# A hybrid decoder trunk: the cast of each weight block prepared ahead waits for the mark that releases the next load

## The chip, the cores and the metric

The kernel runs on one core of a Trainium2 chip. The metric is the time of one execution on the device in microseconds (us), as the median of several runs. Engines are called by the profile's names: PE (matrix engine), PEld (its weight loads), DVE (vector), ACT (scalar), POOL (GpSimd) and SP (here only a queue of DMAs). Each engine takes its own queue in order.

## The reference

The program computes two layers on x of 1024 tokens by 1024 features, all in float32:

```
for i in range(2):
    mix = hgrn2_mixer(x, ...) if i == 0 else conformer_conv_mixer(x, ...)
    x = layer_norm(ALPHA * x + mix, ln_mix_g[i], ln_mix_b[i])
    ff = jnp.square(jax.nn.relu(x @ ffn_w1[i])) @ ffn_w2[i]
    x = layer_norm(ALPHA * x + ff, ln_ffn_g[i], ln_ffn_b[i])
```

The first mixer is a gated linear recurrence with four projections and an output projection. The second has a pointwise projection to 2048 features, a sigmoid gate, a causal depthwise convolution of 31 taps, a layer norm, a silu and a second pointwise projection. Each MLP goes from 1024 to 4096 features and back. What must be seen here is that the order of the work is: mixer A, first MLP (up, down), mixer B (pointwise, convolution, pointwise), second MLP.

## The kernel before, in words

**Products.** Every float32 operand of a large product is split into a high half (a cast to the narrower type fp32r, on ACT) and a low half (the operand less its high half, a subtraction on DVE). PE then makes three products: high by high, high by low, low by high. A slot of 8 KB in each partition holds both halves, `slot[:, 0]` high and `slot[:, 1]` low.

**The first MLP.** Its two matrices are multiplied by a seven-product scheme for 2x2 blocks of blocks; the forms (sums of blocks) are taken in the order `ORDER = (1, 2, 6, 5, 7, 3, 4)`. In the up part (class `Up`, PE's `ps<-x1f,fw`) there are 8 columns c of 7 forms, each of 24 matmuls of 128x512. A product's result leaves PSUM by a copy `c` on ACT (L1266) or by an addition on DVE. In the down part (`down_all`, PE's `ps<-dw,dh`) the outer loop goes over the forms, the inner one over 8 blocks c, again 24 matmuls each, six for each of four row groups `gi`. Behind the last block of a form the four sums are accumulated into `y` (`into`), in two tiles of four token rows. The last form, 4, does its first two blocks alone and the other six together by `gi`; in it rows of `y` are normalised (`to_conv`), transposed on PE (`turn`: four transposes into a PSUM bank, then a cast on ACT and a subtraction on DVE into `xa`) and become the input of the pointwise product that follows.

**Weights prepared ahead.** During the first MLP the kernel also splits 38 blocks of weights of later stages, 512 KB each, and stores both halves to HBM (`ready`), so that they can be loaded as they are. The function `spare` (L1434 to L1452) does one step of it. It is called at the end of a form's split (`Slots.count`, L95 to L99), in the up part for 3 forms of 8 and in the down part for 6 of 8. There is one slot `spare` and one load buffer `next`, claimed behind the first column of the up part. A step has these parts:

- the mark: a DVE copy (L1440) of one element of the low half just made into `now`, a small tile of the tag `ss`, of which there are four buffers in turn;
- if a block has been loaded: its cast on ACT (L1443), its subtraction on DVE, and the two stores by SP (L1447);
- if blocks are left: a POOL copy of the mark into the first column of `next` (L1450), and SP's load into `next` (L1451), which is thereby held until the mark is made and the previous block is out of `next`.

So the mark paces the loads. The memory of `spare` and `next` is given to other tiles when the down part ends.

**Other users of the queues.** POOL also issues the DMAs that add up blocks of weights in `sum_w` (L421, L423) during the up part; each such issue waits for the DMA before it. SP's queue carries the loads of `dr` (raw weights of the down part), of `dh` (its already split activations, then split again from `hf`), and the stores of `ready`.

**What sets the order.** All instructions are recorded and then ordered for each engine by a scheduler that estimates when each could run. An instruction added at one place can therefore shift the order of others on every engine.

Of the kernel before, what the change touches and what calls it, by code (L numbers as in the profile page):

```python
# [268 lines left out]
def body(ctx, tc, d, out):  # L269
    nc = tc.nc  # L270
# [1163 lines left out]
    def spare(after):  # L1434

        if not hold:
            return
        slot, raw = hold
        now = stat.tile([P, 2, 4], F32, tag="ss", name="ss")[:, 0, :1]
        nc.vector.tensor_copy(out=now, in_=after)  # L1440
        if staged:
            key = staged.pop()
            nc.scalar.copy(out=slot[:, 0].bitcast(F32R), in_=raw)  # L1443
            vector.tensor_tensor(out=slot[:, 1].bitcast(F32R), in0=raw, in1=slot[:, 0], op=ALU.subtract)
            ready[key] = tuple(dram.tile([P, 1024], F32, name=f"ready{len(ready)}_{i}") for i in range(2))
            for i in range(2):
                nc.sync.dma_start(out=ready[key][i], in_=slot[:, i])  # L1447
        if ahead:
            name, at = ahead.pop(0)
            nc.gpsimd.tensor_copy(out=raw[:, :1], in_=now)  # L1450
            nc.sync.dma_start(out=raw, in_=d[name][at])  # L1451
            staged.append((name, at))  # L1452

    fw = Forms(nc, vector, slots((144, 152, 48, 112, 120), "fw"), raws(run(192, 4, 4)), raws(run(160, 2, 4), "sum"), spare, 3, range(44))
    fw.todo = [[(blocks("w1q", 0, c), 2 if c < 2 else 0)] for c in range(NFC)]
    up = Up()
# [24 lines left out]

    y = [view(32 + 16 * h, (NTB, D), F32, "y") for h in range(2)]
    fw = Slots(nc, vector, slots([112, 120, 144, 152, 128, 136, 168], "dw"), raws([192, 196, 200, 204, 160, 164], "dr"), spare, 6, range(10, 50))
    fh = Slots(nc, vector, slots([0, 8, 16, 24, 96, 104, 176], "dh"))
    g, b = gain(184, "ln_ffn", 0)
# [472 lines left out]
```

## Time and profile before

| | before |
|---|---|
| median of 3 runs | 2057.86 us (2054.11 to 2058.38) |
| the profiled execution | 2059.69 us |
| its span in the profile | 2057.9 us |
| granted clock of PE, mean | 0.998 |
| first MLP, up part | about 513 to 828 us of the span |
| first MLP, down part | 827.88 to 1136.09 us |
| first pointwise product of mixer B | from 1136.09 us |

A row of a timeline gives the start, the length, the engine, the line, the operation, output and inputs, shape and count of a group of like instructions; in brackets stands how long the engine had been idle before it and what ended that, in us. L204 is a helper through which most instructions go, so those groups are told apart by the names of their tiles. In a window's row each engine's busy time has its number of instructions behind it. A group of waits gives, after the two sides of the wait, the sum of the idle time in us, how often, and the longest.

### The profile page before, as it was taken

To read this page: it belongs to the slowest core of one execution; us is meant where nothing else is said; L and a number is where in the kernel's file an instruction comes from. 1 tells how busy PE (TensorE), PEld (TensorE's weight loads), DVE (VectorE), ACT (ScalarE), POOL (GpSimd) and SP (SyncE) were. 2 spreads that over 40 slices of the span, in tenths; PEclk is the share of its full clock that TensorE was granted. 3 is DMA by queue.
4 is the path that set the end of the run, shared out by engine and by line. 5 is a ranking of instruction groups with operands and counts; after the bars stand their busy time and mean duration, and the time that the engine had idled before them with its cause. 6 is when DMAs were issued, how large, how long until landed. Compare 5 with 4: busy or idle time off the path is not lost. (4 is left out here: it accounts for less than half of the span.)

```text
span 2057.9 us, 29631 instructions
## 1 busy us (share of the span) xinstructions
PE 2026.5 (98%) x11144; PEld 1670.6 (81%) x11144; DVE 1487.4 (72%) x1978; ACT 1092.0 (53%) x1725; POOL 392.1 (19%) x393
## 2 busy tenths in 40 slices
PE   8999999999999999999999999999999999999998
PEld 7888887788787888888888888888888887888886
DVE  8698887877966665666567898889589666754456
ACT  5456565631654555444443776488625555443343
POOL 0112222111100000000001699079110000100002
PEclk9999999999999999999999999999999999999999
DMA  4788989842689786999998854587759778995542
GB/s 187 221 200 228 261 240 252 268 187 82 180 295 307 243 286 224 372 338 325 338 336 301 308 185 184 194 330 272 255 215 343 241 231 297 392 294 197 194 154 102
DMA packets 183944, 517.55 MB, mean 251 GB/s; under 512 B 17912, under 2 KB 49784, under 8 KB 182776
## 3 DMA queue, kind: packets, MB, share of 16 engines
q1 hardware_dynamic: 168312, 456.93, 61.8%
q0 software_dynamic: 15488, 58.72, 12.3%
q8 instruction: 87, 1.43, 0.3%
q14 instruction: 57, 0.47, 0.1%
HBM read 380.85 MB, written 201.85 MB: 283 GB/s over the span
## 5 line engine op out<-in xcount | busy, mean ns | idle before, releaser
L204 PE MATMUL ps<-dw,dh 128*128 128x512 f32 x2688 | 611.1, 389 | 0.0
L204 PEld LDWEIGHTS ps<-dw,dh 128*128 128x128 f32 x2688 | 504.2, 188 | 104.6 <-DVE dh L204 0.2
L204 PE MATMUL ps<-x1f,fw 128*128 128x512 f32 x1344 | 309.7, 392 | 4.6 <-ACT c L1266 2.5
L204 PEld LDWEIGHTS ps<-x1f,fw 128*128 128x128 f32 x1344 | 252.5, 189 | 60.3 <-ACT c L1266 3.6
L204 PE MATMUL ps<-xf,fs 128*128 128x512 f32 x1008 | 250.0, 399 | 3.7 <-issue 2.0
L204 POOL TENSOR_TENSOR cb<-cb,prod 128x512 f32<-128x512 f32 x168 | 223.1, 1337 | 12.5 <-ACT prod L1589 2.0
L204 DVE TENSOR_TENSOR dh<-dh 128x1024 fp32r<-128x1024 f32 x112 | 136.5, 1222 | 116.1 <-ACT dh L72 112.7
L204 PEld LDWEIGHTS ps<-xf,fs 128*128 128x128 f32 x1008 | 185.1, 189 | 43.3 <-issue 2.2
L204 DVE SCALAR_TENSOR_TENSOR ps<-u,par,ps 128x512 f32<-128x512 f32 x296 | 206.1, 749 | 11.0 <-ACT ps L1601 9.5
L204 PE MATMUL ps<-xa,wa 128*128 128x512 f32 x864 | 203.0, 392 | 0.1
L72 ACT CAST dh<-dh 128x1024 fp32r<-128x1024 f32 x112 | 117.4, 1051 | 156.0 <-DMA dh<-hf 148.9
L204 PEld LDWEIGHTS ps<-xa,wa 128*128 128x128 f32 x864 | 160.3, 188 | 33.2 <-ACT ha L1331 0.3
L72 ACT CAST dw<-dr 128x1024 fp32r<-128x1024 f32 x112 | 117.3, 1052 | 131.0 <-PE ps L204 115.3
L204 DVE TENSOR_TENSOR dw<-dr,dw 128x1024 fp32r<-128x1024 f32 x112 | 136.3, 1222 | 69.5 <-ACT dw L72 68.4
L1589 ACT ACTIVATE prod<-u,par 128x512 f32<-128x512 f32 x168 | 119.8, 726 | 37.1 <-POOL cb L204 36.7
L518 POOL TENSOR_TENSOR mv<-mv,nhalf 128x1 f32<-128x1 f32 x32 | 42.2, 1321 | 404.8 <-DVE mv L204 394.5
L1450 POOL COPY next<-ss 128x1 f32<-128x1 f32 x38 | 18.9, 497 | 414.5 <-DVE spare L204 255.1
L204 PE MATMUL ps<-w,oT 128*128 128x512 f32 x384 | 89.9, 392 | 1.3 <-ACT oT L932 0.8
L204 PE MATMUL ps<-xb,wa 128*128 128x512 f32 x384 | 91.1, 393 | 0.0
L204 DVE TENSOR_TENSOR spare<-next,spare 128x1024 fp32r<-128x1024 f32 x38 | 46.5, 1224 | 60.4 <-ACT spare L1443 60.3
L204 PE MATMUL ps<-vw,xf 128*128 128x512 f32 x336 | 79.9, 400 | 5.9 <-ACT vw L435 5.3
L204 PEld LDWEIGHTS ps<-w,oT 128*128 128x128 f32 x384 | 71.4, 188 | 16.6 <-ACT oT L932 1.2
(249 smaller groups left out, 2955.9 us busy)
## 6 DMA issues: line engine op xcount, KB each, us to landing
wa<-ready SPq DMA_DIRECT2D x140, 512.0 KB, 4.6
dh<-hf SPq DMA_DIRECT2D x112, 512.0 KB, 5.0
sum_w<-in_w_dram POOLq DMA_DIRECT2D x40, 1024.0 KB, 10.6
ready<-spare SPq DMA_DIRECT2D x76, 512.0 KB, 5.3
raw<-in_w1q_dram SPq DMA_DIRECT2D x66, 512.0 KB, 4.4
dr<-sum_w SPq DMA_DIRECT2D x64, 512.0 KB, 5.7
hf<-ht SPq DMA_DIRECT2D x112, 256.0 KB, 5.1
dr<-in_w_dram SPq DMA_DIRECT2D x48, 512.0 KB, 4.6
```

The costliest lines, as they stand in the source:

```text
L72: self.nc.scalar.copy(out=slot[:, 0, c], in_=raw[:, c])
L204: return op(*args, **kw)
L518: nc.gpsimd.tensor_tensor(out=dst, in0=src, in1=nhalf[:, :n], op=ALU.pow)
L1450: nc.gpsimd.tensor_copy(out=raw[:, :1], in_=now)
L1589: nc.scalar.activation(tp, u[:, k : k + HT], AF.Copy, scale=tap(j, k))
```

## The change

One line is added in `spare`, as the first of the part that deals with a loaded block:

```
         if staged:
             key = staged.pop()
+            nc.gpsimd.tensor_copy(out=slot[:, 0, :1], in_=now)
             nc.scalar.copy(out=slot[:, 0].bitcast(F32R), in_=raw)
             vector.tensor_tensor(out=slot[:, 1].bitcast(F32R), in0=raw, in1=slot[:, 0], op=ALU.subtract)
```

POOL copies the mark into the first column of the slot's high half. The cast that follows overwrites that column, so it has to come after the copy, and the copy after the mark. It also has to come after the store of the block that was in the slot. Lines behind it are one higher in the changed kernel: the load's copy is L1451, the load L1452. There are 38 such copies more on POOL, one for each block.

On POOL, first MLP, up part, before (`sum_w` are the blocks added up by DMA, `next<-ss` the copy that lets a load go):

```order
L423 DMA sum_w_5415<-sum_w_5415 128x1024 x2
L1450 COPY next<-ss 128x1 x3
L421 DMA sum_w_5882<-in_w_dram 128x2x1024
L1450 COPY next<-ss 128x1
L423 DMA sum_w_5882<-sum_w_5882 128x1024 x2
```

On POOL at the same place, changed (`spare<-ss` is the copy that lets a cast go):

```order
L421 DMA sum_w_5885<-in_w_dram 128x2x1024
L1443 COPY spare<-ss 128x1
L1451 COPY next<-ss 128x1
L423 DMA sum_w_5885<-sum_w_5885 128x1024
L1443 COPY spare<-ss 128x1
L423 DMA sum_w_5885<-sum_w_5885 128x1024
L1451 COPY next<-ss 128x1
```

The copies for casts now stand between the issues of `sum_w` too.

On DVE, end of the first MLP's down part, before. The rows begin at the first accumulation into `y` behind form 3; `dw_7171` is the slot of the second block of form 4, `ss_8674` and `ss_8712` are marks, `mv`, `bs` the statistics of the normalisation:

```order
L204 TENSOR_TENSOR y_7168<-y_7168,ps_70 128x512 x2
L204 TENSOR_TENSOR spare_5428<-next_5429,spare_5428 128x1024
L204 BN_STATS bs_9006<-y_7168 128x6
L204 BN_STATS bs_9214<-y_7168 128x6
L204 TENSOR_SCALAR mv_8998<-mv_8998 128x1
L204 TENSOR_TENSOR y_7169<-y_7169,ps_70 128x512
L1440 COPY ss_8674<-dw_7171 128x1
L204 BN_AGGR mv_9009<-bs_9006 128x2
L204 TENSOR_TENSOR y_7169<-y_7169,ps_70 128x512
L204 TENSOR_TENSOR dh_7197<-dh_7197 128x1024
L1440 COPY ss_8712<-dw_7172 128x1
L204 TENSOR_TENSOR dw_7171<-dr_7184,dw_7171 128x1024
```

On DVE at the same place, changed. Here `dw_7193` and `dw_7183` are the slots of the first and second block of form 4; the first eleven rows from the first accumulation into `y`:

```order
L204 TENSOR_TENSOR y_7180<-y_7180,ps_70 128x512
L204 TENSOR_TENSOR dw_7193<-dr_7195,dw_7193 128x1024
L204 TENSOR_TENSOR y_7180<-y_7180,ps_70 128x512
L204 TENSOR_SCALAR mv_9036<-mv_9036 128x1
L204 BN_STATS bs_9044<-y_7180 128x6
L204 BN_STATS bs_9252<-y_7180 128x6
L204 TENSOR_TENSOR y_7181<-y_7181,ps_70 128x512
L204 BN_AGGR mv_9047<-bs_9044 128x2
L204 TENSOR_SCALAR mv_9036<-mv_9036 128x1
L204 SCALAR_TENSOR_TENSOR y_7180<-y_7180,mv_9036,ln_ffn_g_7213 128x1024
L204 TENSOR_TENSOR y_7181<-y_7181,ps_70 128x512
```

And the eleven behind them, to the subtraction that makes the low half of `dw_7183`:

```order
L204 TENSOR_SCALAR mv_9047<-mv_9047 128x1
L204 SCALAR_TENSOR_TENSOR y_7180<-y_7180,mv_9047,ln_ffn_g_7213 128x1024
L204 TENSOR_TENSOR spare_5428<-next_5429,spare_5428 128x1024
L204 TENSOR_TENSOR dh_7209<-dh_7209 128x1024
L204 SCALAR_TENSOR_TENSOR y_7180<-y_7180,mv_9036,ln_ffn_b_7215 128x1024
L204 SCALAR_TENSOR_TENSOR y_7180<-y_7180,mv_9047,ln_ffn_b_7215 128x1024
L204 TENSOR_TENSOR dh_7210<-dh_7210 128x1024
L1440 COPY ss_8711<-dw_7183 128x1
L204 TENSOR_TENSOR dh_7212<-dh_7212 128x1024
L204 TENSOR_TENSOR xa_7219<-ps_70,xa_7219 128x4x128
L204 TENSOR_TENSOR dw_7183<-dr_7196,dw_7183 128x1024
```

This subtraction was the 13th instruction from the first accumulation and is now the 22nd. Behind it come another subtraction for `xa`, one for `spare`, a third for `xa`, two marks, and then the subtraction for the next block, `dw_7184`.

On PE at this place, before (`dw_7181` and `dw_7171` are the first two blocks of form 4, the others the six that are taken together; `ident,y` are transposes):

```order
L204 MATMUL ps_70<-dw_7181,dh_7200 128x512 x24
L204 MATMUL ps_70<-dw_7171,dh_7192 128x512 x24
L204 MATMUL ps_70<-dw_7172,dh_7193 128x512 x9
L204 MATMUL ps_70<-dw_7174,dh_7194 128x512 x6
L204 MATMUL ps_70<-dw_7175,dh_7195 128x512
L204 MATMUL ps_70<-dw_7172,dh_7193 128x512 x5
L204 MATMUL ps_70<-dw_7174,dh_7194 128x512 x6
L204 MATMUL ps_70<-dw_7175,dh_7195 128x512
L204 MATMUL ps_70<-dw_7172,dh_7193 128x512 x2
L204 MATMUL ps_70<-ident_74,y_7168 128x128 x8
```

On PE at this place, changed (`dw_7191` is the last block of form 3):

```order
L204 MATMUL ps_70<-dw_7191,dh_7210 128x512 x24
L204 MATMUL ps_70<-dw_7193,dh_7212 128x512 x20
L204 MATMUL ps_70<-dw_7183,dh_7204 128x512 x4
L204 MATMUL ps_70<-ident_74,y_7180 128x128 x12
L204 MATMUL ps_70<-dw_7183,dh_7204 128x512 x19
L204 MATMUL ps_70<-ident_74,y_7180 128x128 x4
L204 MATMUL ps_70<-dw_7183,dh_7204 128x512
L204 MATMUL ps_70<-dw_7184,dh_7205 128x512 x8
L204 MATMUL ps_70<-dw_7186,dh_7206 128x512 x6
```

The first transposes of `y` moved from behind 30 matmuls of the third to fifth block into the second block. Over the whole down part PE's order was 1230 matmuls, 8 transposes, 31, 8, 57, 8, 24, 8 and 2 matmuls; it is now 1180, 12, 19, 4, 86, 8, 30, 8 and 29.

More of the change, by code (lines that the diff above doesn't have):

```diff
@@ L1442, in spare @@
             key = staged.pop()
+            nc.gpsimd.tensor_copy(out=slot[:, 0, :1], in_=now)
             nc.scalar.copy(out=slot[:, 0].bitcast(F32R), in_=raw)
```

## The prediction

> **What bounds the kernel now.** I read the page first. PE, the matrix engine, carries the time:
>
> ```profile
> span 2057.9 us, 29631 instructions
> PE 2026.5 (98%) x11144; PEld 1670.6 (81%) x11144; DVE 1487.4 (72%) x1978; ACT 1092.0 (53%) x1725; POOL 392.1 (19%) x393
> ```
>
> PE is idle for 2057.9 - 2026.5 = 31.4 us in all. Any gain has to come out of these; any loss is a new PE wait. The windows say how much lies where the edit acts (window, length, PE, PEld, DVE, ACT, POOL busy, granted clock, DMA share, GB/s):
>
> ```profile
> 580.00:740.00 160.00, 157.38 (x689) 128.67 (x689) 103.11 (x124) 87.68 (x129) 7.58 (x14) 1.00 0.83 279
> 740.00:1080.00 340.00, 340.00 (x1502) 281.62 (x1501) 208.81 (x230) 171.19 (x195) 13.42 (x31) 1.00 0.88 317
> 1080.00:1140.00 60.00, 60.00 (x282) 49.82 (x281) 44.60 (x61) 23.26 (x32) 9.58 (x17) 1.00 0.85 307
> 1140.00:1300.00 160.00, 159.56 (x741) 131.74 (x741) 139.38 (x214) 116.84 (x193) 133.97 (x106) 1.00 0.59 217
> ```
>
> In the first MLP's up part (580 to 740) PE lacks 2.62 us; from 740 to 1140 nothing. So the edit can win at most 2.6 us there, and every wait it makes from 740 on is a plain loss. The timeline of PE shows the 2.6:
>
> ```profile
> 659.21 36.08 PE L204 MATMUL ps<-x1f,fw 128*128 128x512 f32 x156 [1.25 <-ACT c L1266]
> 695.85 13.90 PE L204 MATMUL ps<-x1f,fw 128*128 128x512 f32 x60 [0.56 <-ACT c L1266]
> 709.97 13.89 PE L204 MATMUL ps<-x1f,fw 128*128 128x512 f32 x60 [0.22 <-DVE c L204]
> 724.36 25.93 PE L204 MATMUL ps<-x1f,fw 128*128 128x512 f32 x113 [0.50 <-ACT c L1266]
> ```
>
> That is 2.53 us, mostly waits for ACT's copies `c` that free a PSUM bank. ACT's timeline and its group of waits (us, times, longest) say why ACT was late:
>
> ```profile
> 656.68 1.05 ACT L1443 CAST spare<-next 128x1024 fp32r<-128x1024 f32 x1 [4.28 <-DMA next<-in_wpw_dram]
> 657.64 1.04 ACT L72 CAST fw<-raw 128x1024 fp32r<-128x1024 f32 x1
> 658.58 1.07 ACT L1266 COPY c<-ps 128x512 f32<-128x512 f32 x2
> ACT spare L1443 <- DMA next<-in_wpw_dram: 38.0, 18, 4.3
> ```
>
> ACT runs its queue in order. The spare cast at 656.68 had stood 4.28 us waiting for its load, with the `c` copies behind it.
>
> **The change part by part.** It adds 38 one-element POOL copies. Each waits for the mark (a DVE copy of the tail of the form just made) and the cast waits for it. Before, a cast waited for its load only and could stand in ACT's queue a whole mark early.
>
> *Price of the copy.* POOL's 38 copies of the same kind (count: min/median/max ns), the mark, the costliest one, and POOL's two largest blocks of the up part:
>
> ```profile
> L1450 POOL COPY next<-ss x38: 183/186/2317, 580.2 to 1118.9; 128x1 f32<-128x1 f32 x38
> 652.03 0.16 DVE L1440 COPY ss<-fw 128x1 f32<-128x1 f32 x1
> 1098.45 2.32 POOL L1450 COPY next<-ss 128x1 f32<-128x1 f32 x1 [1.99 <-DVE spare L204]
> 636.32 0.85 POOL L423 DMA_DIRECT2D sum_w<-sum_w  x1 [11.65 <-DMA sum_w<-in_w_dram]
> ```
>
> 38 x 0.186 = 7.1 us on an engine busy 19%: nothing by itself. A copy can lie between 0.18 and 2.32 us after its mark, and behind a queued sum_w issue it can wait up to 11.65.
>
> *A, the up part: gain.* The cast that ran at 656.68 will go at about 652.03 + 0.16 + 0.19 = 652.4, since a load asked for a mark earlier has long landed. ACT then has its copies done before PE asks. I take -2.3 of the 2.53: most of the idle goes, and the sum_w issues may keep one piece. Bounds: 0 (every copy comes as late as the load did) and -2.5. A loss here is the second rival.
>
> *B, the end of the down part: a new wait.* The rows of order in the section on the change show it: the sub that makes the low half of the second block of form 4 (dw_7183; before, dw_7171) stands 22nd from the first `y` accumulate, where it was 13th. The reason is the four-deep ring `ss`: the mark of this block takes a buffer that a POOL copy behind a spare sub has to give back, and the copies are now two per mark. The low half is needed after 4 of the block's matmuls. Before:
>
> ```profile
> 1059.76 47.09 PE L204 MATMUL ps<-dw,dh 128*128 128x512 f32 x207
> 1106.68 1.03 PE L204 MATMUL ps<-ident,y 128*128 128x128 f32 x8
> 1107.47 7.29 PE L204 MATMUL ps<-dw,dh 128*128 128x512 f32 x31
> 1085.12 0.69 DVE L204 TENSOR_TENSOR y<-y,ps 128x512 f32<-128x512 f32 x1 [0.45 <-PE ps L204]
> 1092.34 1.21 DVE L204 TENSOR_TENSOR dw<-dr,dw 128x1024 fp32r<-128x1024 f32 x1
> ```
>
> A matmul is 47.09/207 = 0.2275 us. 50 of them stood between the need and the transposes (20 of the block, then 30), so PE needed the half at 1106.68 - 50 x 0.2275 = 1095.3, and had it at 1093.55: 1.7 us to spare. Now the DVE path, priced from its rows:
>
> ```profile
> 1088.56 1.28 DVE L204 BATCH_NORM_STATS2 bs<-y 128x6 f32<-128x512 f32 x2
> 1093.47 0.14 DVE L204 TENSOR_SCALAR mv<-mv 128x1 f32<-128x1 f32 x1
> 1093.53 1.27 DVE L204 SCALAR_TENSOR_TENSOR y<-y,mv,ln_ffn_g 128x1024 f32<-128x1024 f32 x1
> 1104.24 3.48 DVE L204 TENSOR_TENSOR dw<-dr,dw 128x1024 fp32r<-128x1024 f32 x3
> 1132.99 2.36 DVE L204 SCALAR_TENSOR_TENSOR y<-y,b_pw 128x1024 f32<-128x1024 f32 x2 [2.03 <-DMA b_pw<-in_b_pw_dram]
> ```
>
> Start to start: wide subs (3.48 - 1.22)/2 = 1.13; wide scalar_tensor_tensor 2.36/2 = 1.18; 512-wide ones 0.6 (1.28 for two); small ones 0.06 (1093.47 to 1093.53). The 22 rows are 5 wide subs, 4 wide scalar_tensor_tensor, 7 of 512, 5 small, and the sub itself: 5.65 + 4.72 + 4.2 + 0.3 + 1.21 = 16.1, and 0.2 for hops. PE meanwhile has, from the matmul that releases that `y`, 18 + 20 + 4 matmuls and 12 transposes. Eight transposes take 1107.47 - 1106.68 = 0.79, so 42 x 0.2275 + 12 x 0.099 = 9.55 + 1.19 = 10.7. Wait: 16.3 - 10.7 = 5.6. A second path is longer. The dh sub two places ahead needs a load whose slot PE frees after 38 of those matmuls (8.6). The load and ACT's cast are in
>
> ```profile
> dh<-hf SPq DMA_DIRECT2D x112, 512.0 KB, 5.0
> 1094.71 1.06 ACT L72 CAST dh<-dh 128x1024 fp32r<-128x1024 f32 x1 [0.26 <-DMA dh<-hf]
> ```
>
> 8.6 + 5.0 + 1.06 + 1.13 + 0.6 + 1.21 = 17.6, so the wait is 6.9; with a hop 7.0, which I take. Bounds 5.6 (first path alone) and 9 (7.0 and 2 more, should SP's issue of that load stand behind the store of a spare whose cast now waits for a copy of up to 2.32).
>
> *C, the block behind it.* The sub of dw_7184 stands behind the third xa sub, whose four transposes PE itself issues 19 matmuls later:
>
> ```profile
> 1107.32 1.07 ACT L1045 CAST xa<-ps 128x512 fp32r<-128x512 f32 x2 [0.71 <-PE ps L204]
> 1108.78 1.27 DVE L204 TENSOR_TENSOR xa<-ps,xa 128x512 fp32r<-128x512 f32 x2
> ```
>
> DVE: 19 x 0.2275 + 0.40 (four transposes) + 0.54 + 0.64 + 0.12 (two marks) + 1.21 + 0.2 = 7.4; PE: 4.32 + 0.40 + 4 x 0.2275 = 5.6. Wait 1.8. Bounds 1.5 (no hop) and 4.1 (the mark's buffer waits for a copy of 2.32).
>
> *D, the last transposes of the part.* PE's transposes of the first row of `y` now stand 59 matmuls and 16 transposes (15.0 us) before the end of the part; before, 1136.09 - 1128.41 = 7.7:
>
> ```profile
> 1128.41 1.03 PE L204 MATMUL ps<-ident,y 128*128 128x128 f32 x8
> 1136.09 15.24 PE L204 MATMUL ps<-xa,wa 128*128 128x512 f32 x66
> 1122.69 1.27 DVE L204 SCALAR_TENSOR_TENSOR y<-y,mv,ln_ffn_b 128x1024 f32<-128x1024 f32 x1
> ```
>
> That row was ready at 1123.96, with 4.45 to spare; 7.3 earlier would be 2.9 short, but B and C have made PE 8.8 late while DVE goes on. I take 0.5; bounds 0 and 2.9.
>
> Sum: 7.0 + 1.8 + 0.5 - 2.3 = +7.0. The profiled execution took 2059.69 (span 2057.9), 1.8 above the median of the three runs; 2059.69 + 7.0 = 2066.7, or 2064.9 against the median of 2057.86. All ends together: 5.6 + 1.5 + 0 - 2.5 = +4.6 and 9 + 4.1 + 2.9 - 0 = +16.
>
> A rule that speaks against these sizes: the Trainium skill, VectorE: DVE Perf Modes, section The DRAIN you can't avoid, says that behind each operation the pipe empties for about its length less 266 ns before the next starts. The trace disagrees: by the rule the three subs at 1104.24 would start 2.2 us apart; they start 1.13 apart. Another, SBUF — State Buffer, section SBUF: two separate sides, says that a GpSimd operation and a DVE one with two SBUF inputs lock each other out for a whole instruction. By it a mark's copy would cost at most one sub, and the upper end of C would be 3.0; the copy of 2.32 is longer than a sub of 1.21, so the trace does not bear that limit out.
>
> **The rivals.** *In time after all: not slower.* PE reaches the low half of dw_7183 with it there; the gain of A stands alone: 2057.86 - 2.3 = 2055.6. It decides if the 22 rows are through within 10.7 us of the first `y`, 0.49 us each, or if the `y` accumulates do not wait for PE. For it: the sub had 1.7 to spare before. Against it: at 1085.12 the accumulate did wait for PE, and the wide rows take 1.13. Chance 0.18. With that, the order of all that follows changes too: 28 of the 31.4 idle us lie before 580 or after 1300, and if another 2 of them go it is 2053.6, faster by over 0.2%. Chance 0.08.
>
> *Marks behind sum_w.* The copies for casts stand in POOL's queue between the issues L421 and L423, one of which waited 11.65 us. A cast held there stands in ACT's queue with `c` copies behind it, and PE waits when a copy is over 36 matmuls (8.2 us) late (12 to a product, four banks, so three products lie between): about 11.65 - 8.2 = 3.5 in place of the gain of 2.3, so +5.8: 2070.7; half of it with one bank more at hand, 2068. Chance 0.10.
>
> *Half of it.* B is its lower end, C finds the mark there, D is nothing and A full: 5.6 + 0 - 2.5 = +3.1, 2061.0. Chance 0.12.
>
> *The drain rule.* By it the path of 22 rows would take some 30 us, the wait 19, the time 2077. The three subs speak against it: 0.02.
>
> **How the numbers follow.** The forecast holds 0.50, its own range 2062.0 to 2068.0. A measurement of this kernel tells changes above 0.2%, 4.1 us, from none. Slower: 0.50 + 0.10 + 0.02 = 0.62. Same: 0.18 + 0.12 = 0.30. Faster: 0.08. The range goes from the first rival (2055.5) to the sum_w rival's middle (2069.5); what is left out is 0.08 below, 0.02 of the drain, the dear half of sum_w and the far ends of B to D, some 0.18.
>
> **What would show it.** Right: in the profile after, PE has idle rows of about 7 and 2 us put down to DVE's dw, between 1090 and 1120; the spare casts' waits for `next` shrink from 38 us to a few, with waits for POOL in their place; PE's idle from 580 to 740 is below 0.5; PE's transposes of y[0] stand in a group of 12. Wrong: PE without a wait from 740 to 1140 (B to D fail), or new waits for `c` between 580 and 740 (A fails, sum_w holds).

## The result and the profile after

The changed kernel takes 2066.28 us (median of 6 runs, 2064.21 to 2066.98) where the kernel before, run beside it, takes 2058.05 (6 runs). The ratio is 1.0041, with a 95% interval of 1.0028 to 1.0053: 8.2 us slower. The profiled execution took 2066.48 us, 6.8 more than that of before.

The page of the changed kernel:

```profile
span 2064.7 us, 29733 instructions
PE 2025.8 (98%) x11144; PEld 1671.2 (81%) x11144; DVE 1490.5 (72%) x1978; ACT 1093.3 (53%) x1725; POOL 412.7 (20%) x431
```

PE is busy as long as before (0.7 us less). Its idle time went from 31.4 to 2064.7 - 2025.8 = 38.9 us. POOL has its 38 copies more. The windows tell in which stage the idle time lies:

```profile
580.00:740.00 160.00, 158.73 (x699) 130.76 (x698) 104.68 (x128) 87.21 (x128) 10.89 (x24) 1.00 0.83 278
740.00:1080.00 340.00, 338.74 (x1493) 279.85 (x1493) 207.13 (x227) 172.54 (x195) 22.78 (x53) 1.00 0.87 317
1080.00:1140.00 60.00, 52.87 (x238) 42.81 (x237) 41.23 (x56) 22.10 (x29) 14.80 (x14) 0.94 0.78 275
1140.00:1300.00 160.00, 160.00 (x738) 132.74 (x737) 139.62 (x212) 112.20 (x185) 134.20 (x115) 1.00 0.60 221
```

Idle in the up part: 1.27 us, where it was 2.62. Then 1.26 where there was none, and 7.13 in the 60 us at the end of the down part, where there was none. Idle time is not all of a loss, since PE can also run slower. The first matmul of each stage tells the whole: the up part's starts at 513.13 us before and at 513.24 changed, the down part's at 827.88 and 825.74, the pointwise product's at 1136.09 and 1145.91. So the up part became 2.25 us shorter and the down part 12.0 us longer. Behind it the changed program took 918.8 us and the one before 921.8; in the profiles of the other runs this stretch takes 919.5 to 927.5 us, so the 3.0 are no more than its scatter. The timeline of PE at the end of the down part:

```profile
1079.52 15.75 PE L204 MATMUL ps<-dw,dh 128*128 128x512 f32 x68 [0.40 <-DVE dw L204]
1096.83 1.09 PE L204 MATMUL ps<-ident,y 128*128 128x128 f32 x8 [1.56 <-DVE y L204]
1101.65 1.09 PE L204 MATMUL ps<-ident,y 128*128 128x128 f32 x4 [3.73 <-DVE xa L204]
1102.69 6.04 PE L204 MATMUL ps<-dw,dh 128*128 128x512 f32 x19
1108.92 19.77 PE L204 MATMUL ps<-dw,dh 128*128 128x512 f32 x86
1130.53 1.09 PE L204 MATMUL ps<-ident,y 128*128 128x128 f32 x8 [1.84 <-DVE y L204]
```

The 8 and 4 transposes are the group of 12 that the order showed; 19 matmuls of the second block of form 4 follow. DVE in the same stretch, from the first `y` accumulate to the subtraction that PE needs (the row at 1101.42) and beyond:

```profile
1085.79 0.69 DVE L204 TENSOR_TENSOR y<-y,ps 128x512 f32<-128x512 f32 x1
...
1095.50 2.47 DVE L204 SCALAR_TENSOR_TENSOR y<-y,mv,ln_ffn_b 128x1024 f32<-128x1024 f32 x2
1099.68 1.22 DVE L204 TENSOR_TENSOR dh<-dh 128x1024 fp32r<-128x1024 f32 x1 [0.50 <-ACT dh L72]
1100.82 0.68 DVE L204 TENSOR_TENSOR xa<-ps,xa 128x512 fp32r<-128x512 f32 x1
1101.42 1.21 DVE L204 TENSOR_TENSOR dw<-dr,dw 128x1024 fp32r<-128x1024 f32 x1
1104.32 0.68 DVE L204 TENSOR_TENSOR xa<-ps,xa 128x512 fp32r<-128x512 f32 x1
...
1105.17 1.22 DVE L204 TENSOR_TENSOR dw<-dr,dw 128x1024 fp32r<-128x1024 f32 x1
```

From 1085.79 to 1102.63 DVE worked through its 22 instructions in 16.8 us with one wait of 0.50, for the load of `dh`. PE went on with its 19 matmuls at 1102.69, the moment the subtraction ended. So the wait at the end of the down part is DVE's queue, as forecast, though the profile puts the 3.73 down to `xa` and not to `dw`: PE's last four transposes of the group stand first, and want the bank that the `xa` subtraction at 1100.82 empties, one place ahead of the subtraction for `dw`.

### The profile page after: what moved, and what is told of

It is laid out like the page before. It is cut to its first block, busy times and chain, and to the rows that moved or that the text cites. A ratio compares the mean times of both kernels' runs of the same rounds, so it can differ in the third digit from the quotient of the medians.

```text
span 2064.7 us, 29733 instructions
## 1 busy us (share of the span) xinstructions
PE 2025.8 (98%) x11144; PEld 1671.2 (81%) x11144; DVE 1490.5 (72%) x1978; ACT 1093.3 (53%) x1725; POOL 412.7 (20%) x431
## 4 chain that ended last, share of the span: by engine, by line
PE 71%; DMA 14%; DVE 6%; issue 4%; ACT 3%; POOL 2%; SPq 0%; DVEq 0%; POOLq 0%; ACTq 0%
PE ps L204 71%; DMA sum_w<-in_w_dram 6%; DMA y<-kept 1%; DMA dh<-hf 1%; DMA hf<-ht 1%; DMA ready<-spare 1%; POOL cb L204 1%; DMA vr<-in_wv_dram 1%; DMA next<-in_w_dram 1%; DMA raw<-in_w1q_dram 1%; DMA next<-in_w1q_dram 1%; DVE xf L204 0%; DVE vr L204 0%; DVE qk L204 0%; DMA raw<-in_wout_dram 0%
## 5 line engine op out<-in xcount | busy, mean ns | idle before, releaser
L204 PEld LDWEIGHTS ps<-xb,wa 128*128 128x128 f32 x384 | 71.1, 188 | 14.3
L204 PEld LDWEIGHTS ps<-vw,xf 128*128 128x128 f32 x336 | 64.2, 192 | 21.2 <-ACT vw L435 5.2
```

Source lines behind the costliest of these rows:

```text
L204: return op(*args, **kw)
```

## The experiments

Every ratio is to the kernel before on the same chip, each with its 95% interval. On those chips the kernel before took 2062 to 2065 us.

**e1: the copy in the up part only.**

```
+            if len(ready) < 12:
+                nc.gpsimd.tensor_copy(out=slot[:, 0, :1], in_=now)
```

> The added copy only for the first 12 prepared blocks, those of the up part. In the order the end of the down part is back as before: the second block of form 4 has its low half from the 13th instruction behind the first y accumulate, and PE's counts are 1230, 8, 31, 8, 57, 8, 24, 8, 2. Theory 1 (the place of that subtraction in DVE's queue costs the 7 us): the loss is gone and only the up part's gain of 1.35 us is left, 2056.7 us, ratio 0.9993; PE has no idle row from 740 to 1140. Theory 2 (38 casts that wait on POOL cost by themselves, wherever they stand): 12/38 of 8.2 us, 2060.6. Theory 3 (the whole order is shuffled and the loss sits in many places): anything between 2054 and 2066, with idle rows at new places.

Measured 0.9987 (0.9977 to 0.9997). PE in the stretch in question:

```profile
1079.70 25.55 PE L204 MATMUL ps<-dw,dh 128*128 128x512 f32 x112
1137.65 16.22 PE L204 MATMUL ps<-xa,wa 128*128 128x512 f32 x64 [2.48 <-DMA wa<-ready]
```

PE went without a wait to the end of the down part; its wait of 2.48 comes behind it, for a block that had been prepared. The loss is gone. Theory 2, by which the casts' waits cost by number, gives 2060.6/2058.05 = 1.0012, outside the interval, and falls. The wait for `wa` is 0.71 in e11, which is the same kernel, 0.46 in e4 and 1.22 in e9, and the profile of before has none; whether the edit brings it is not shown.

**e2: the copy in the down part only.**

```
+            if len(ready) >= 12:
+                nc.gpsimd.tensor_copy(out=slot[:, 0, :1], in_=now)
```

> The added copy only from the 13th prepared block on, in the down part. The order at the end of the down part is as in the changed kernel (22nd instruction, PE 1180, 12, 19, 4, 86). Theory 1: PE idle of 7.1 us between 1080 and 1140 as in the changed kernel, none of the up part's gain: 2058.05 + 8.2 + 1.35 = 2067.6 us, ratio 1.0046. Theory 2: 26/38 of 8.2 us, 2063.7. Theory 3: as for the run above.

Measured 1.0040 (1.0026 to 1.0053), the whole loss. The same rows of PE:

```profile
1082.71 15.75 PE L204 MATMUL ps<-dw,dh 128*128 128x512 f32 x68 [1.26 <-DVE dw L204]
1100.55 1.84 PE L204 MATMUL ps<-ident,y 128*128 128x128 f32 x8 [2.09 <-DVE y L204]
1105.10 1.09 PE L204 MATMUL ps<-ident,y 128*128 128x128 f32 x4 [2.71 <-DVE xa L204]
```

The two parts of the change act in different places: the copies of the up part do not bring the loss, and those of the down part bring it alone. That their effects simply add is not shown; the intervals allow it.

**e3: 32 marks in flight.** Every cast still waits for its mark; only the marks' buffers are more.

```
-        now = stat.tile([P, 2, 4], F32, tag="ss", name="ss")[:, 0, :1]
+        if not marks:
+            t = stat.tile([P, 2, 4], F32, tag="ss", name="ss")
+            marks.extend(t[:, i, j : j + 1] for i in range(2) for j in range(4))
+        now = marks.pop(0)
```

> The change as it is, but eight marks share one tile of the tag ss, so 32 marks are in flight in place of 4; every cast still waits for its mark through POOL. In the order the low half of the second block of form 4 is the 11th instruction behind the first y accumulate. Theory 1 in its strong form (the ring of four holds the mark, and with it the subtraction, behind POOL): the waits of 1.56, 3.73 and 1.84 us at the end of the down part go and the up part's gain stays, 2056.7 us (2054 to 2058). Theory 2 (the casts' wait itself costs): no change from the changed kernel, 2066. If the marks' ring is only half of it, 2060 to 2062 with a wait for y left.

Measured 0.9992 (0.9982 to 1.0002), 4.9 thousandths below the changed kernel. The windows:

```profile
740.00:1080.00 340.00, 339.24 (x1497) 280.62 (x1496) 209.62 (x235) 170.82 (x194) 33.68 (x51) 1.00 0.89 318
1080.00:1140.00 60.00, 60.00 (x282) 50.06 (x281) 41.05 (x57) 29.12 (x43) 16.50 (x27) 1.00 0.78 280
```

No idle time at the end of the down part, with all 38 waits of the change in place. In the order all 43 marks now stand before the first `y` accumulate behind form 3, where the changed kernel has 38 of them there, as the kernel before has. A mark reads the low half that is in a slot, so the next subtraction into that slot stands behind it; with four buffers it also stands behind the chain of prepared blocks. This is the run that decides against the casts' wait. For the marks' ring it speaks together with e4 and e7: the subtraction stands 22nd with four buffers and copies of the mark, 13th with four buffers and none (before, e4), and 11th with 32, with the copies or without.

**e4: the copy without the mark.** The copy takes a constant; the cast still waits for POOL and POOL for the slot.

```
-            nc.gpsimd.tensor_copy(out=slot[:, 0, :1], in_=now)
+            nc.gpsimd.tensor_copy(out=slot[:, 0, :1], in_=ident[:, :1])
```

> 38 POOL copies as in the change, each held by the stores of the slot's previous block and holding the cast, but of a constant in place of the mark: the copies without the wait for the mark. The order at the end of the down part is as before (13th). Theory 1: no wait at the end of the down part, and the up part as before since casts stand early again: 2058 us, ratio 1.000. Theory 2 (copies and casts' wait on POOL cost by themselves): 2062 to 2066.

Measured 1.0002 (0.9987 to 1.0017). The 38 copies cost nothing that can be measured. Nor is a gain to be seen in the up part without the mark: its window has 2.40 us of idle time, near the 2.62 of before.

```profile
580.00:740.00 160.00, 157.60 (x684) 129.05 (x684) 101.63 (x123) 86.50 (x127) 11.50 (x25) 0.99 0.83 281
```

**e5: four banks for the transposes.** This asks who owns the wait of 3.73, the bank or DVE's subtraction.

```
-                rings["aux"] = bank((4, 5))
+                rings["aux"] = bank((4, 5, 6, 7))
```

> The change, and the transposes of y at the end of the down part take turns in four PSUM banks (4, 5, 6, 7) in place of two, up to the last form's second row group. In the order PE now has 16 transposes in a row where it had 12, and DVE's subtraction for the second block of form 4 is still the 22nd instruction behind the first y accumulate. Theory 1 (that subtraction sets the end of the wait): the idle row of 3.73 us put down to xa goes, but an idle row of about as much comes back in front of dw's matmuls, put down to DVE's dw; total as the changed kernel, ratio to before 1.004. Rival (PE waits for a free bank, the transposes' two banks being the bound): 3.7 us less than the changed kernel, ratio 1.002.

Measured 1.0018 (1.0005 to 1.0031), which is the rival's number. The trace says otherwise:

```profile
1094.72 2.29 PE L204 MATMUL ps<-ident,y 128*128 128x128 f32 x16 [1.55 <-DVE y L204]
1101.10 30.15 PE L204 MATMUL ps<-dw,dh 128*128 128x512 f32 x119 [4.10 <-DVE dw L204]
```

The wait for the bank went and a wait of 4.10 for `dw` came in its place: 5.65 us together where there were 5.29. So the subtraction sets the end of that wait, whatever the banks. What was saved is elsewhere: the wait of 1.84 before the next transposes is gone, since in this order those stand behind 119 matmuls. By that alone the ratio would be 1.0041 - 1.84/2058 = 1.0032, just above the interval's end; the rest of the difference is within what the two intervals leave open. The down part, from its first matmul to that of the pointwise product, took 319.0 us against 320.2 in the changed kernel, so that of the 12.0 lost only 1.2 came back. The total pointed to the wrong theory, the rows tell them apart.

**e6: the last six casts free.**

```
+            if len(ready) < 32:
+                nc.gpsimd.tensor_copy(out=slot[:, 0, :1], in_=now)
```

> The change without the added copy for the last 6 prepared blocks, those whose casts run while form 4 goes on. In the order the subtraction for the second block of form 4 is still late, the 23rd behind the first y accumulate. Theory 1: the loss stays, ratio 1.004 (1.003 to 1.005), with PE idle of 5 to 8 us between 1080 and 1140. Rival (the last casts' own wait for POOL at that place, and the stores behind it, make the loss): ratio 0.999 to 1.000 and no such idle.

Measured 1.0028 (1.0014 to 1.0043), and the waits stand where they stood, among them

```profile
1097.37 1.09 PE L204 MATMUL ps<-ident,y 128*128 128x128 f32 x8 [1.94 <-DVE y L204]
1102.14 1.08 PE L204 MATMUL ps<-ident,y 128*128 128x128 f32 x4 [3.68 <-DVE ss L1440]
1131.16 1.10 PE L204 MATMUL ps<-ident,y 128*128 128x128 f32 x8 [1.80 <-DVE y L204]
```

So it is not what the last casts wait for while form 4 runs. The shift needs the copies for the 13th to 32nd blocks, earlier in the down part (e1, with the first 12 alone, has none), and is only felt at the end.

**e7 and e8: the ring by itself, and with the up part's copies.** e7 is the kernel before with e3's edit; e8 is e3 with e1's condition.

> The kernel before with eight marks to a tile of the tag ss, 32 in flight, and no added copy. The subtraction for the second block of form 4 is the 11th instruction behind the first y accumulate. Theory 1: PE had no wait in the down part, so the ring alone wins nothing there, ratio 1.000 (0.999 to 1.001). Rival (the ring of four costs something elsewhere too, and explains the 0.9992 of the changed kernel with 32 marks): ratio 0.998 to 0.999.

> Eight marks to a tile, and the added copy only for the first 12 prepared blocks: the up part's gain with the early marks of the down part. By theory 1 the two do not add anything to the up part's gain: ratio 0.9987 to 0.9994. If the two gains add (the ring's own and the up part's), 0.998 or less.

Measured 0.9990 (0.9977 to 1.0003) and 0.9982 (0.9970 to 0.9995). The 0.9990 of e7 is where its two theories meet and decides between neither, so the ring may win something by itself, and e3's 0.9992 may hold a part of that. e8 is the only one besides e1 whose interval lies below 1: 3.7 us under the kernel before by the ratio, 2.6 by the medians. Its up part shows no gain: PE's idle time from 580 to 740 is 2.96 us there. Whether the two gains add cannot be said from these intervals, which overlap.

**e9, e10, e11: the load's copy on DVE.** In the changed kernel one cast of the up part still waited 3.84 us for its load, and I thought that the load's own POOL copy, behind a `sum_w` issue, was the reason. e9 is e1 with that copy on DVE in the up part, e10 is e8 with it, and e11 is e1 again, beside them.

```
-            nc.gpsimd.tensor_copy(out=raw[:, :1], in_=now)
+            (nc.vector if len(ready) < 13 else nc.gpsimd).tensor_copy(out=raw[:, :1], in_=now)
```

> As e1 (the added copy for the first 12 blocks only), and in the up part the copy that lets a load go runs on DVE in place of POOL, so that it no longer stands behind the sum_w issues in POOL's queue. The order at the end of the down part is as before. Theory (the up part's gain fell short because the load itself was late, its POOL copy having stood behind a sum_w issue until 647): the cast that waited 3.84 us for its load waits under 1 us, PE's idle row put down to ACT's c near 655 to 661 goes, and PE's idle from 580 to 740 is 0.3 us or less where e1 has 1.9; ratio 0.998. Rival (the waits for c have another cause, DVE's own subtractions and sums): the cast no longer waits, PE's idle stays above 1 us, ratio 0.9987.

> e8 (eight marks to a tile, the added copy for the first 12 blocks) with the load's copy of the up part on DVE as in e9. If the load's lateness is what was left of the up part's idle time: 1 to 2 us less than e8, ratio 0.9975. If not: as e8, 0.998 to 0.999.

> The kernel of e1 on the chip of e9 and e10, as their neighbour: ratio 0.9987 (0.998 to 0.9995).

Measured 0.9999 (0.9987 to 1.0011), 0.9998 (0.9984 to 1.0011) and 0.9992 (0.9982 to 1.0002). The copy on DVE wins nothing: in e9 PE's idle time from 580 to 740 is 5.02 us, where the theory had 0.3 or less. In e9 the copy, the load it lets go (SP), and the cast:

```profile
645.51 0.15 DVE L1452 COPY next<-ss 128x1 f32<-128x1 f32 x1
650.63 0.42 SPq L1453 DMA_DIRECT2D next<-in_wpw_dram  x1
662.38 1.04 ACT L1445 CAST spare<-next 128x1024 fp32r<-128x1024 f32 x1 [5.12 <-DMA next<-in_wpw_dram]
```

The copy was done at 645.66 and SP issued the load at 650.63, 5.0 us later. In SP's queue the load stands behind a load of `raw` (issued at 647.99), the previous block's stores and a store of `hf`. My theory for the short gain falls: with POOL's copy out of the way it is SP's queue that holds the load. The rival, that DVE's work alone makes the waits for `c`, is not shown by that either, since the cast still waited.

**The two stages in all profiles.** The down part took 319.0 to 322.0 us in the changed kernel, e2, e5 and e6, where the subtraction stands 22nd or 23rd, and 308.2 to 309.7 us in the kernel before and the eight other runs. That is a clear gap of 9 to 14 us. The up part took 312.5 to 314.6 us in the seven profiles with copies of the mark there and the load's copy on POOL, and 313.9 to 315.8 us in the four with no copy of the mark there. These overlap, and e1 and e11, one kernel, differ by 0.8 us (by idle time, 1.90 against 0.48). So a gain there is likely, about 1 us on average, but its size is not settled by the profiles.

## Why the prediction came out, step by step

The forecast was 2064.9 us, 7.0 more than before; 8.2 were measured. The first step, that any new wait from 740 on is a plain loss, held. The terms did not all hold:

**A, the up part, had the right direction, and one step of it failed.** Forecast -2.3. In this pair of profiles the idle time of the window fell by 1.35 and the stage by 2.25 us. By run times e1 and e11 put the whole gain at 0.8 to 1.3 thousandths, 1.6 to 2.7 us, with one of the intervals reaching above 1. The size fits, within a scatter as large as itself. The step that failed is "a load asked for a mark earlier has long landed". The prediction's own row speaks against it: the cast at 656.68 had waited for its load until then, 4.5 us after the mark was made. The same cast in the changed kernel, ACT's two groups of waits, the copy that let it go, and what PE still waited for:

```profile
ACT spare L1444 <- POOL spare L1443: 23.9, 7, 7.2
ACT spare L1444 <- DMA next<-in_wpw_dram: 16.2, 7, 3.8
656.01 0.37 POOL L1443 COPY spare<-ss 128x1 f32<-128x1 f32 x1 [8.11 <-DMA ready<-spare]
659.41 1.05 ACT L1444 CAST spare<-next 128x1024 fp32r<-128x1024 f32 x1 [3.84 <-DMA next<-in_wpw_dram]
667.81 158.10 PE L204 MATMUL ps<-x1f,fw 128*128 128x512 f32 x696 [1.06 <-DVE c L204]
```

The forecast of 652.4 left out a second wait as well: the copy ran only at 656.01, held by the store of the slot's previous block and not by the mark. (The 0.18 to 2.32 us that the prediction took for the distance from the mark are the copy's own length.) Of POOL's idle times before these copies, 25 end with such a store and 7 with a mark. The casts' waits for these loads fell from 18 times and 38.0 us to 7 and 16.2. But 23.9 us of waits for POOL came, and the waits for loads from the two other matrices rose from 19.7 to 32.3 us, so ACT stood about as long in front of its casts as before, 72.4 us against 74.1. Of PE's 1.27 us left, 0.21 is a wait for ACT's `c` behind the cast at 659.41, and 1.06 one for an addition into `c` on DVE. In DVE's queue that addition stands behind the subtraction of the same block, for which DVE was idle for 4.16 us; that the 1.06 goes back to it is not shown.

**B, the wait for the low half, was right in place and mechanism.** Forecast 7.0 with bounds of 5.6 and 9. PE ended its matmuls at 1079.52 + 15.75 = 1095.27 and began the 19 at 1102.69. Of these 7.42 us, 1.19 are what 12 transposes take without a wait, so 6.2 are lost (5.3 in the two idle rows, the rest in transposes slower than that). Both paths were sized well: 16.8 us for the 22 instructions (16.1 forecast), and the load landed so that the `dh` subtraction began 0.50 us after DVE was free, 17 us where 17.6 were forecast. SP issued that load 8.6 us behind the first `y`, as forecast, and it landed in 4.2 us where I took 5.0 (SP's issue and ACT's cast):

```profile
1094.39 0.32 SPq L90 DMA_DIRECT2D dh<-hf  x1
1098.60 1.04 ACT L72 CAST dh<-dh 128x1024 fp32r<-128x1024 f32 x1 [2.33 <-DMA dh<-hf]
```

The reason that I gave for the order is right in the ring (e3, e4) and wrong in two details. The mark in question is not this block's: it reads what the slot held before. And the two copies per mark at that place do not hold it: without them there (e6) the order stays late. By which of the earlier blocks the scheduler arrives at it was not isolated.

**C did not come at all.** Forecast 1.8; PE runs the 86 matmuls from 1108.92 without a wait. I took the third `xa` subtraction to read the four transposes that PE issues 19 matmuls later. The DVE row at 1104.32 shows that it reads the last four of the group of 12, so the subtraction for dw_7184 was done at 1106.39, 2.5 us before PE came to that block.

**D came larger, and by another path.** Forecast 0.5 with bounds of 0 and 2.9; measured 1.84, the row at 1130.53. The forecast let DVE go on while PE was late, and that failed. The first row is from before, the others from the changed kernel:

```profile
1116.20 1.06 ACT L1443 CAST spare<-next 128x1024 fp32r<-128x1024 f32 x1
1123.59 1.05 ACT L1444 CAST spare<-next 128x1024 fp32r<-128x1024 f32 x1 [8.29 <-DMA next<-in_w1q_dram]
1124.55 1.05 ACT L1083 ACTIVATE dr<-y 128x1024 f32<-128x1024 f32 x1
1129.19 1.28 DVE L204 SCALAR_TENSOR_TENSOR y<-y,mv,ln_ffn_b 128x1024 f32<-128x1024 f32 x1 [0.58 <-POOL mv L518]
```

ACT's pass for the normalisation of that row (L1083) stands right behind the cast of a prepared block, before as well (at 1117.17). Now this cast waited 8.29 us for its load, and the row of `y` was ready at 1130.47, 6.5 us later than before. POOL had let this load go at 1116.12; in the kernel before it had let go the one in the same place at 1109.09. The added copy is not what held the cast: in e6, which has none there, the cast waits 8.12 us for its load and PE 1.80. C and D together were forecast at 2.3.

**Not in the sum:** 1.26 us of waits between 740 and 1080. One, 0.86 for a first block of `dh`, is in e1 (0.29), in e2 (1.20) and in e7 (1.10), which has no added copy, so the lateness of that block is not owed to the copies. The other, 0.40 before 1079.52, stands in e2 (1.26), e5 (0.69) and e6 (1.34) and not in e1 and e3, so it goes with the late order. And PE ran slower for some time after its wait, below: about 1.7 us.

**The sum was near partly by luck.** For the down part 7.0 + 1.8 + 0.5 = 9.3 us were forecast and 12.0 came: B's 6.2, D's 1.84, the 1.26 of other waits and the 1.7 of slow matmuls, with about 1 us that was not traced to a row. That C did not come made up for a part of what was left out.

**The rivals.** "In time after all" is out by the row of 3.73 and by e2. "Half of it" gives 2061.0, a ratio of 1.0015, below the interval; but two of its four conditions came nearly true, C at nothing and B at 6.2, between its 5.6 and the 7.0 forecast, and it fails by D and by what was in no sum. "Marks behind sum_w" did not come: the up part gained. The drain rule is out, 16.8 us against some 30. Of the signs, the group of 12 transposes came, and the waits for POOL in place of some for `next`. PE's waits came too, but were put down to `y` and `xa`, and the last lies at 1130. PE's idle time from 580 to 740 was 1.27, not below 0.5, and the casts' waits for `next` did not shrink to a few us.

## What to carry to other kernels

A one-element copy that only paces something cost nothing here by its own time (e4); look at what its buffer couples, for a mark taken from a small ring ties the queue of the engine that writes it to whoever reads it last. Where a scheduler sets the order, list it before and after and count the instructions between a wait's start and the instruction that ends it: here the count, 22 instead of 13, and the durations of the trace gave this wait to within 1 us. A change of a few us is read better from the length of the stage that it acts on than from the whole time: here two groups of runs lay 9 us apart in the down part, while the part behind it scatters by nearly as much. And an engine that runs its queue in order passes a wait on to whatever stands behind it, as the cast in D did. When the same time is put down to another name after an edit, as with the bank in e5, the edit removed the label and not the cause.

## What the runs showed of the hardware

After some of its waits PE runs at half clock. In the changed kernel, before and after 1102.69 (the last columns are the granted clock, DMA share and GB/s):

```profile
1100.00:1103.00 3.00, 1.35 (x5) 1.03 (x6) 3.00 (x4) 1.51 (x3) 0.00 (x0) 0.50 0.13 52
1103.00:1106.00 3.00, 3.00 (x8) 2.34 (x8) 2.97 (x6) 0.64 (x2) 0.19 (x1) 0.54 0.67 197
1106.00:1109.00 3.00, 3.00 (x17) 2.46 (x16) 2.78 (x5) 0.04 (x1) 0.97 (x1) 1.00 0.99 359
```

Eight matmuls in 3 us at a clock of 0.54, then 17 with some transposes among them at 1.00. The 19 matmuls took 6.04 us, 1.7 more than 19 x 0.2275 = 4.32. A shorter wait did the same in e1, 2.48 us at the start of the pointwise product:

```profile
1137.65:1140.00 2.35, 2.35 (x6) 1.87 (x7) 0.55 (x2) 1.68 (x3) 0.42 (x3) 0.50 0.94 295
1140.00:1143.00 3.00, 3.00 (x13) 2.48 (x12) 0.59 (x4) 3.00 (x7) 0.19 (x2) 0.88 1.02 415
```

There 64 matmuls took 16.22 us, 1.7 more than at 0.2275. The wait of 1.84 before 1130.53 was not followed by it:

```profile
1131.00:1134.00 3.00, 3.00 (x18) 2.54 (x17) 1.81 (x2) 2.02 (x3) 0.00 (x0) 1.00 1.02 401
```

Length alone does not decide it, since behind the 1.90 us that e1 waited at 655 the clock was down as well:

```profile
657.00:660.00 3.00, 3.00 (x9) 2.31 (x8) 0.24 (x1) 0.59 (x1) 0.28 (x1) 0.60 1.03 407
```

Nor does a wait of 2.35 us always do it: behind the one before 663.96 in e9 the clock stayed at 1.00.

```profile
664.00:667.00 3.00, 3.00 (x13) 2.50 (x14) 2.35 (x4) 1.34 (x2) 0.00 (x0) 1.00 0.96 351
```

So of PE's waits of 1.8 to 2.5 us here some were followed by half clock and some were not. In the two cases reckoned here it cost 1.7 us on top of the wait's length. What decides is not shown. The Trainium skill, TensorE: Matmul & The Clock Gate, Part 1, puts a drop to half rate behind an idle window of about 3.4 us. The half rate agrees with the 0.50 of these rows; the length does not, since 1.90 and 2.48 us were enough.
